# Hybrid encoder block on one Trainium2 core: channel layout at the head, forget gate behind the gate chunks, gate stores on GpSimd, two gate chunks moved out of attention

## The chip, the cores and the metric

The kernel runs on one core of one Trainium2 chip. The core has five engines, each with an instruction stream of its own: TensorE (PE: matrix products, with a separate slot PEld for loading weights), VectorE (DVE), ScalarE (ACT), GpSimd (POOL) and SyncE (SP). They work on an on-chip buffer and on accumulators; data come and go through DMA queues, which any of SP, ACT and POOL can feed. The metric is the time of one execution on the device in microseconds (us); lower is better. A measurement gives the median of several executions.

## The reference

One block of a streaming encoder, 1,024 tokens behind 16 learned ones ("meta"), so 1,040 positions of 1,024 channels, in float32. What matters here, cut from the reference:

```python
h = concatenate([meta, x], axis=1)                      # (1, 1040, 1024)
xn = _rmsnorm(h, norm_mix_g)                            # x * rsqrt(mean(x^2) + eps) * g
proj = xn @ w_in                                        # 1024 -> 512+512+512+8+512+2048
q, k, v, f_logit, u, gates = split(proj, SPLITS)
y_a = _forgetting_attention(q, k, v, f_logit, b_forget) @ w_attn_out    # 8 heads of 64
z   = gelu(_s5(u, ...))                                 # diagonal complex state space model, 32 groups of 16
zg  = z @ w_glu
y_s = zg[..., :1024] * sigmoid(zg[..., 1024:])
g   = sigmoid(gates)
h   = h + (g[..., :1024] * y_a + g[..., 1024:] * y_s) @ w_o
h   = h + _conv_ffn(_rmsnorm(h, norm_ffn_g), ...)       # 1024 -> 5632, conv of width 3, silu gate, 2816 -> 1024
out = _rmsnorm(h, norm_final_g)[:, 16:]
```

The attention adds F[t] - F[s] to its scores, where F is the running sum of log sigmoid(f_logit + b_forget): that is the forget gate. The meta tokens are dropped from the output.

## The kernel before, in words

**Precision.** TensorE multiplies in a rounded 32-bit format. Every operand is split into a high part and a low remainder, and each product is the sum of three: high by high, high by low, low by high (lines L159 to L161 in `dense_steps`, L327 to L329 in `part`). So a product over 1,024 channels is 8 blocks of 128 channels (KD = 8) times 3 matmuls.

**Stages, in the order of time.** (1) The head: the normalised tokens as features `xhi`, `xlo` (128 channels by position, 8 such blocks), and beside them the projection U for the state space model. (2) The state space model (`ssm`, four quarters of its 32 groups) with eight gate chunks as TensorE's filling. (3) Queries and keys of head pair 0 (`project_qk`), the forget gate (`forget`), the forms of z and the GLU (`load_z`, L219 in the helper for its seven products). (4) Values and the attention, four pairs of heads. (5) Merge, output product, convolutional FFN and last norm; nothing of the change touches these.

**The head.** U has 512 rows (four m of 128) over 1,040 positions, cut into blocks of columns `UBLK` = 272, 256, 256, 256. Block 0 comes from the host in channel layout (`x0t`, channels on partitions) and without the norm: its features are x times the channel's weight `g1T`, and the tokens' norm factor is multiplied in behind the product, on `us` (for which three factor vectors are spread over the partitions by transposes). All other tiles of 128 tokens are loaded in token layout (`load_x`), squared and summed on ScalarE (`norm_factor`), multiplied on VectorE by factor and weight (`features`, L340), transposed on TensorE (L191, eight transposes a tile), and then cut into high (ScalarE, L193) and low parts (VectorE, L129). Block 0's own positions are normalised in this way a second time, later, so that `xhi`, `xlo` can serve the other projections. The weights of U are cut in L355 (`uh`) and the line behind it (`ul`). The results are stored to `u_d` (L394): for odd m by GpSimd, for even m by SP, eight DMAs each.

**The state space model.** `ssm` computes its constants in long rows of small products on VectorE (L1453, L1456, L1459), then for each quarter the tables Gm, Kt, Tm, Vm and Wi: Gm on VectorE, Kt by TensorE from Gm (L1692), Wi by transposes of Vm that ScalarE copies (L1714). The chain of a quarter loads U from `u_d`, multiplies by Wi (L1730), scans, and stores Y to `y_d`. The constants are tied behind the feature product called `ready`.

**Gate chunks.** A chunk is 128 of the 2,048 gate rows: 3 blocks of 342 positions times 24 matmuls, 72 in all. Chunks 8 to 15 belong to the state space branch and are computed in stage 2, chunks 0 to 7 to attention. The weights of chunk 8 have places of their own (`gate0`, shown as g, g0 and the like). For a chunk of stage 2 (`wchunk(act=True)`) GpSimd issues the load, ScalarE casts the high part (L146) and writes its negative as the low one, and GpSimd issues a DMA (L136, `lo_by_dma`) that loads the weights once more and adds them to it. The sigmoids go to `g_d` by a DMA that ScalarE issues (L444).

**Order.** The body is written as a program; a scheduler places instructions on each engine, and `after(a, b)` pins a behind b on the order alone, without a semaphore. DMAs of one engine's queue are issued in that engine's order. Attention (`GA`, `fill`, `HOOKS`) spreads the filling of a pair evenly over its score and value steps: the next pair's queries and keys (2 x 3 x 24 matmuls) and `GA[pair]` gate chunks (72 each), here 2, 1, 1 and 3; the last of the eight is computed behind it. These chunks take tanh, GpSimd's affine step and a store by SP.

**The forget gate.** Its weights are 8 columns (`wf`, high and low side by side in 64 columns). SP issues their load behind the 32 loads of z, GpSimd cuts them (its subtraction is recorded at L129), and three blocks of 16 matmuls (L518) follow the queries and keys. ScalarE, VectorE and GpSimd then turn them into F, which is stored to `f_d` and loaded by the attention.

Of the kernel before, what the change touches and what calls it, by code (L numbers as in the profile page):

```python
# [50 lines left out]
def block_kernel(ctx, tc, x, meta, g1, x0t, g1t, w_q, w_k, w_v, w_f, w_u, w_g, b_f, w_ao, lam_d, bw_d, cw_d,  # L51
# [118 lines left out]
    def norm_factor(pl, src, n, bufs=10, sq=None):  # L170
# [3 lines left out]
        S.activation(sq[:n], src, AF.Square, accum_out=ss[:n])  # L174
        va = pl.tile([P, 1], F, tag="vr", name="vr", bufs=3)
        V.tensor_scalar(va[:n], ss[:n], 1.0 / D, EPS, ALU.mult, ALU.add)
# [110 lines left out]
    xa = [sp.tile([P, 4, UN], F, tag="tq", name="xa", bufs=3) for _ in range(2)]  # L287
    g1T = n1.tile([P, KD], F, name="g1T")
    S.dma_start(g1T, g1t)
    S.dma_start(xm, meta)  # L290
# [9 lines left out]
    for j in range(4):  # L300
        load(xa[j // 2][:, 2 * (j % 2):2 * (j % 2) + 2], x0t[:, 2 * j:2 * j + 2])
        load(uraw[j], w_u[:, 2 * j:2 * j + 2])
    xts = [sp.tile([P, D], F, tag=tag, name="xt", bufs=n) for tag, n in (("Wi", 2), ("Gm", 2), ("sy", 3)) for _ in range(n)]
    g1B = xts.pop(4)
    g1_load = S.dma_start(g1B, g1.partition_broadcast(P))

    place = dict(zip((3, 4, 1, 2, 5, 6), xts))
    place[0] = xm

    def load_x(i):  # L310
        load(place[i], x[P * (i - 1):P * i])

    for i in range(1, 7):
        load_x(i)
# [19 lines left out]
    def factors(i):  # L334
        n = TILES[i][1]
        return norm_factor(n1, place[i][:n], n)

    def features(i, rs, behind=None):
        t, n = TILES[i]
        xn = V.scalar_tensor_tensor(out=place[i][:n], in0=place[i][:n], scalar=rs[:n], in1=g1B[:n],  # L340
                                    op0=ALU.mult, op1=ALU.mult)
# [5 lines left out]
    for j in range(4):  # L347
        for k in (2 * j, 2 * j + 1):
            src, hi = xa[j // 2][:, k % 4], xhi[:, k, :UN]
            cp_ = S.activation(hi, src, AF.Copy, scale=g1T[:, k:k + 1])  # L350
            if k == 1:
                after(g1_load, cp_)
            V.scalar_tensor_tensor(out=xlo[:, k, :UN], in0=src, scalar=g1T[:, k:k + 1], in1=hi.bitcast(F),
                                   op0=ALU.mult, op1=ALU.subtract)
        S.copy(uh[j], uraw[j])  # L355
        split_lo(V, ul[j], uraw[j], uh[j])
        for m in range(4):
            for k in (2 * j, 2 * j + 1):
                part(first[m], m, k, 0, UN)
    for i in (7, 8):  # L360
        place[i] = sp.tile([P, D], F, tag="Tm", name="xt", bufs=2)
        load_x(i)

    rs0 = [factors(i) for i in range(3)]
    tp = t_ps()
    for i, rs in enumerate(rs0):
        t, n = TILES[i]
        rb = sp.tile([P, P], F, tag="wi", name="rb", bufs=2)
        V.tensor_copy(rb[:n], rs[:n].broadcast_to([n, P]))
        PE.transpose(tp[:, t:t + n], rb[:n], ident[:n, :n])  # L370
    rsB = sp.tile([P, UN], F, tag="wr", name="rsB", bufs=2)
    S.copy(rsB, tp[:, :UN])
    for i in (3, 4):
        ready = features(i, factors(i))
    n_log = len(ssm_log)
    for m in range(4):
        V.tensor_tensor(us[m][:, :, :UN // CH], by_chunks(first[m][:, :UN]), by_chunks(rsB), ALU.mult)

    for b, (t, n) in enumerate(UBLK[1:]):
        if b:  # L380
            for i in (3 + 2 * b, 4 + 2 * b):
                last = features(i, factors(i))
        for m in range(4):
            ps = mm_ps()
            for k in range(KD):
                part(ps, m, k, t, n)
            S.copy(us[m][:, :, t // CH:(t + n) // CH], by_chunks(ps[:, :n]))
        if b == 2:
            for i in range(3):
                features(i, rs0[i], last)  # L390
# [34 lines left out]

    st_g = ExitStack()
    gp_ = pool(st_g, "gates", side="right")

    okeep = {}

    def gate_chunk(i, pl, tanh):
# [3 lines left out]
        for t, n in QBLK:  # L435
# [5 lines left out]
            else:  # L441
                gs = pl.tile([P, LQ // 3], F, tag="gs", name="gs", bufs=2)
                S.activation(gs, ps[:, :n], AF.Sigmoid)
                S.dma_start(g_d[P * i:P * i + P, t:t + n], gs)  # L444
# [7 lines left out]
    for i in range(KD, 2 * KD):  # L452
# [3 lines left out]
    st_f = ExitStack()  # L456
    fp = pool(st_f, "fgate", side="right")
    fraw = fp.tile([P, KD, H], F, name="fraw")
    wf = fp.tile([P, KD, 64], R, name="wf")
    bf = fp.tile([H, 1], F, name="bf")  # L460

    def forget_w():
        SY.dma_start(fraw, w_f)
        SY.dma_start(bf, b_f.unsqueeze(1))
        GP.memset(wf.bitcast(F), 0.0)
        GP.tensor_scalar(wf[:, :, :H], fraw, 1.0, 0.0, ALU.mult, ALU.add)
        split_lo(GP, wf[:, :, 32:32 + H], fraw, wf[:, :, :H])

# [42 lines left out]
    def forget():  # L511

        fl_ = gz.tile([P, L], F, tag="gl", name="fl_", bufs=2)[:H]
        fx = gz.tile([P, L], F, tag="gl", name="fx", bufs=2)[:H]
        for t, n in BLK:
            ps = mm_ps()
            for i in range(KD):
                PE.matmul(ps[:64, :n], wf[:, i, :], xhi[:, i, t:t + n], start=(i == 0), stop=False)  # L518
                PE.matmul(ps[:64, :n], wf[:, i, :], xlo[:, i, t:t + n], start=False, stop=(i == KD - 1))
            S.copy(fx[:, t:t + n], ps[32:32 + H, :n])  # L520
            V.scalar_tensor_tensor(out=fl_[:, t:t + n], in0=ps[:H, :n], scalar=bf, in1=fx[:, t:t + n],
                                   op0=ALU.add, op1=ALU.add)
        V.scalar_tensor_tensor(out=fx, in0=fl_, scalar=-1.0, in1=fl_, op0=ALU.mult, op1=ALU.max)
        S.activation(fx, fx, AF.Exp, scale=-1.0)
        S.activation(fx, fx, AF.Ln, bias=one[:H])
        V.scalar_tensor_tensor(out=fx, in0=fl_, scalar=0.0, in1=fx, op0=ALU.min, op1=ALU.subtract)
        V.tensor_tensor_scan(fl_, one[:H].broadcast_to([H, L]), fx, 0.0, ALU.mult, ALU.add)
        GP.tensor_scalar(fx, fl_, -8.0, 0.0, ALU.mult, ALU.add)
        SY.dma_start(f_d, fx)
        if "f_d" in dbg:  # L530
            SY.dma_start(dbg["f_d"], fx)

# [3 lines left out]
    def load_z():  # L536
        zts = []
        for m in range(4):
# [3 lines left out]
            for g in range(GQ):  # L542
                SY.dma_start(zt[GC * g:GC * g + GC], ym[g])
# [62 lines left out]
    forget_w()  # L606
    qk = qk_tiles(0)
    run(project_qk(0, qk))
    forget()
    st_f.close()  # L610
# [173 lines left out]
    GA = [2, 1, 1, 3]  # L784
# [39 lines left out]
    done = 0  # L824
# [620 lines left out]
def ssm(tc, after, sp, s_ps, ident, u_d, y_d, lam_d, bw_d, cw_d, d_sk, l_dt):  # L1445
# [27 lines left out]
    S.dma_start(ldt, l_dt.partition_broadcast(P))  # L1473

    lam = sm([P, 2, G])
    S.dma_start(lam, lam_d)
# [8 lines left out]
    def rest():  # L1485
# [234 lines left out]
        def chain(qt):  # L1720
# [54 lines left out]
            S.dma_start(y_d[qt], Y)  # L1775
# [61 lines left out]
```

## Time and profile before

| | us |
|---|---|
| median of 3 runs | 1488.93 |
| the runs | 1488.93, 1492.47, 1485.58 |
| the profiled execution: its span | 1485.7 |
| stage 1, 0 to 73.5 | 73.5 |
| stage 2, 73.5 to 195.4 | 121.9 |
| pair 0, queries and keys, and forget gate, 195.4 to 238.0 | 42.6 |
| z and GLU, 238.0 to 325.0 | 87.0 |
| values and what precedes the first scores, 325.0 to 440.5 | 115.5 |
| pairs 0 to 3 of attention | 68.7, 66.8, 65.5, 65.5 |
| the rest, 707.0 to 1485.7 | 778.7 |

The span, from the first to the last instruction of the profiled execution, lies 3.2 us under the median of the runs and inside their spread; differences in the trace are set against this span.

How the rows are read. A row of the timeline is: start in us, duration in us, engine, line, operation, output<-inputs, partitions by elements, count, and in brackets the idle time before it with what ended it. Matmuls overlap, so the pitch between two starts is what one costs, not its duration. A group row is: line, engine, operation, names, shape, count | busy us, mean ns of one | idle time before. A row of stretches is: from:to, length, then the busy time (and instructions) of PE, PEld, DVE, ACT, POOL, then the granted clock of TensorE (1.00 is full), the DMA engines' mean busy share, and GB/s. A row of waits is: who <- what it waited for: us in total, times, longest. A row of DMAs is: output<-input, queue, operation, count, KB each, median us from issue to landing.

### The profile page before, as it was taken

To read this page: it belongs to the slowest core of one execution; us is meant where nothing else is said; L and a number is where in the kernel's file an instruction comes from. 1 tells how busy PE (TensorE), PEld (TensorE's weight loads), DVE (VectorE), ACT (ScalarE), POOL (GpSimd) and SP (SyncE) were. 2 spreads that over 40 slices of the span, in tenths; PEclk is the share of its full clock that TensorE was granted. 3 is DMA by queue.
4 is the path that set the end of the run, shared out by engine and by line. 5 is a ranking of instruction groups with operands and counts; after the bars stand their busy time and mean duration, and the time that the engine had idled before them with its cause. 6 is when DMAs were issued, how large, how long until landed. Compare 5 with 4: busy or idle time off the path is not lost. (4 is left out here: it accounts for less than half of the span.)

```text
span 1485.7 us, 26584 instructions
## 1 busy us (share of the span) xinstructions
PE 1440.4 (97%) x9712; PEld 1358.8 (91%) x9712; DVE 1071.4 (72%) x2173; ACT 712.2 (48%) x1384; POOL 742.1 (50%) x850
## 2 busy tenths in 40 slices
PE   7999997999999999999999999999999999998997
PEld 7989996998899999999888999999999999777886
DVE  6879648881566676647468987888877776788785
ACT  6434675541555665543546534444444445543433
POOL 1311125752456465524863144455544426789766
PEclk9999999999999999999999999999999999999999
DMA  6366571551127342047885135676653215765513
GB/s 246 86 157 157 128 163 50 177 160 43 48 79 178 93 111 90 26 148 256 257 158 185 57 109 141 178 199 188 174 143 100 84 57 180 286 203 148 168 40 114
DMA packets 91032, 206.72 MB, mean 139 GB/s; under 512 B 14651, under 2 KB 25531, under 8 KB 90517
## 3 DMA queue, kind: packets, MB, share of 16 engines
q1 hardware_dynamic: 69380, 159.73, 32.9%
q0 software_dynamic: 15296, 34.63, 13.2%
q10 hardware_dynamic: 6224, 10.65, 1.9%
q8 instruction: 77, 1.26, 0.3%
q14 instruction: 55, 0.44, 0.1%
HBM read 165.90 MB, written 69.35 MB: 158 GB/s over the span
## 5 line engine op out<-in xcount | busy, mean ns | idle before, releaser
L159 PE MATMUL mm<-xhi,whi 128*128 128x342 f32 (+2 forms) x488 | 159.4, 327 | 1.0 <-DVE q L129 1.0
L161 PE MATMUL mm<-xhi,wlo 128*128 128x342 f32 (+2 forms) x488 | 158.3, 325 | 0.0
L160 PE MATMUL mm<-xlo,whi 128*128 128x342 f32 (+2 forms) x488 | 157.7, 324 | 0.0
L1079 POOL TENSOR_TENSOR ov<-ov,og 128x1024 f32<-128x1024 f32 x21 | 51.1, 2434 | 125.6 <-ACT og L1078 121.7
L129 DVE TENSOR_TENSOR sw<-sf,sw 128x512 fp32r<-128x512 f32 x72 | 66.6, 925 | 50.0 <-ACT sw L1070 49.8
L1070 ACT CAST sw<-sf 128x512 fp32r<-128x512 f32 x72 | 44.9, 624 | 106.2 <-POOL sf L1196 74.5
L159 PEld LDWEIGHTS mm<-xhi,whi 128*128 128x128 f32 x488 | 91.9, 188 | 2.1 <-PE sp L714 0.8
L161 PEld LDWEIGHTS mm<-xhi,wlo 128*128 128x128 f32 x488 | 91.8, 188 | 0.3
L160 PEld LDWEIGHTS mm<-xlo,whi 128*128 128x128 f32 x488 | 91.9, 188 | 0.2
L763 ACT CAST th<-tp 128x256 fp32r<-128x256 f32 (+3 forms) x120 | 56.2, 472 | 62.5 <-PE tp L756 30.1
L129 DVE TENSOR_TENSOR tl<-tp,th 128x256 fp32r<-128x256 f32 (+3 forms) x120 | 65.2, 547 | 25.1 <-ACT th L763 23.7
L1196 POOL TENSOR_TENSOR sf<-raw,sf 128x512 f32<-128x512 f32 x36 | 59.1, 1641 | 44.8 <-DVE sw L129 44.7
L1196 POOL TENSOR_TENSOR sf<-raw 128x512 f32<-128x512 f32 x36 | 48.0, 1332 | 66.9 <-DMA raw<-in_w_up_dram 35.9
L221 PE MATMUL mm<-xhi,sw 128*128 128x258 f32 (+1 forms) x288 | 81.0, 281 | 0.0
L219 PE MATMUL mm<-xhi,sw 128*128 128x258 f32 (+1 forms) x288 | 80.8, 281 | 0.0
L220 PE MATMUL mm<-xlo,sw 128*128 128x258 f32 (+1 forms) x288 | 80.7, 280 | 0.0
L728 POOL TENSOR_SCALAR pt<-pt,nm 128x144 f32<-128x144 f32 (+4 forms) x72 | 51.8, 731 | 48.5 <-DVE nm L727 47.5
L1248 DVE SCALAR_TENSOR_TENSOR ov<-hv,cwt,ov 128x1024 f32<-128x1024 f32 x36 | 72.5, 2014 | 0.1
L1070 ACT CAST sw<-raw 128x512 fp32r<-128x512 f32 x70 | 43.0, 621 | 53.3 <-PE sp L221 25.5
L726 ACT ACTIVATE pt<-pt,nm 128x144 f32<-128x144 f32 (+4 forms) x72 | 52.9, 735 | 26.1 <-DVE nm L725 25.7
L719 DVE CUSTOM_DVE_ANT_0 pt<-sp,fb 128x328 f32<-128x328 f32 (+8 forms) x112 | 46.4, 430 | 20.0 <-PE sp L714 11.1
L756 PE MATMUL tp<-ident,pt 128*128 128x128 f32 (+1 forms) x360 | 58.3, 270 | 0.1
(708 smaller groups left out, 5702.1 us busy)
## 6 DMA issues: line engine op xcount, KB each, us to landing
raw<-in_w_up_dram SPq DMA_DIRECT2D x44, 512.0 KB, 3.6
t_d<-in_w_dn_dram POOLq DMA_DIRECT2D x44, 256.0 KB, 7.0
ar<-a_d SPq DMA_DIRECT2D x44, 256.0 KB, 5.1
wr<-t_d SPq DMA_DIRECT2D x44, 256.0 KB, 2.8
a_d<-ov SPq DMA_DIRECT2D x21, 512.0 KB, 2.6
wr<-in_w_dn_dram SPq DMA_DIRECT2D x33, 256.0 KB, 3.8
t_d<-in_w_dn_dram SPq DMA_DIRECT2D x22, 256.0 KB, 4.2
t_d<-t_d SPq DMA_DIRECT2D x22, 256.0 KB, 4.7
```

Source lines behind the costliest of these rows:

```text
L129: return eng.tensor_tensor(out_, src, hi.bitcast(F), ALU.subtract)
L159: yield PE.matmul(ps, whi[:, i, :], ahi[:, i], start=(i == 0), stop=False)
L160: yield PE.matmul(ps, whi[:, i, :], alo[:, i], start=False, stop=False)
L161: yield PE.matmul(ps, wlo[:, i, :], ahi[:, i], start=False, stop=(i == k - 1))
L219: PE.matmul(ps, a[0][:, i], bh, start=(i == 0 and not joins), stop=False, skip_group_check=True)
L220: PE.matmul(ps, a[0][:, i], bl, start=False, stop=False, skip_group_check=True)
L221: PE.matmul(ps, a[1][:, i], bh, start=False, stop=(i == kh - 1), skip_group_check=True)
L756: PE.transpose(tp[:kn, o:o + n], p_[:n, k0:k0 + kn], ident[:n, :n])
L763: S.copy(th[:kn, z:tw], tp[:kn, z:tw])
L1070: S.copy(hi, src)
L1196: sums.append(GP.tensor_tensor(f_, a, b, op))
L1248: V.scalar_tensor_tensor(out=o, in0=h_[:, j:SEQ + j], scalar=cwc(j, m), in1=o, op0=ALU.mult, op1=ALU.add)
```

## The change

It has four parts.

1. *The head in channel layout.* The host hands over all of x in channel layout too, by blocks of U's columns (`xbt`). Tokens are no longer transposed. The token tiles are still loaded, but only for the norm factors; each factor is spread over 128 columns by VectorE and turned by one transpose a tile, and ScalarE copies the result to `spread[b]`. For blocks 2 and 3 VectorE multiplies the whole block by `spread` ahead of the features (`normed_features`, two products of 4 x 256 columns); blocks 0 and 1 go through U without the norm, which is multiplied in on `us` behind it, and are normed and cut a second time later. The first weights and channels come in smaller pieces (`FIRST`). `ready`, behind which the constants of the state space model are pinned, is now the last feature of block 1's second pass.
2. *The forget gate* is loaded by GpSimd early in stage 2 and computed behind the gate chunks, ahead of pair 0's queries and keys; its store goes to GpSimd.
3. *GpSimd's queue* takes over the stores of the sigmoids, of Y, half of the loads of z for m = 3, and three small loads at the start.
4. *Two of attention's gate chunks* (0 and 1) are computed in stage 2, with sigmoid, behind chunks 8 to 15 (`AHEAD` = 2), and `GA` goes from 2, 1, 1, 3 to 1, 1, 0, 3.

```diff
-    S.dma_start(xm, meta)
+    GP.dma_start(xm, meta)
...
+    FIRST = [(0, 1), (1, 1), (2, 2), (4, 2), (6, 2)]
+    for k, n in FIRST:
+        load(xT[0][k // 4][:, k % 4:k % 4 + n], x0t[:, k:k + n])
+        load(uraw[k // 2][:, k % 2:k % 2 + n], w_u[:, k:k + n])
+
+    def load_block(b, tag):
+        xT[b] = [sp.tile([P, 4, UBLK[b][1]], F, tag=tag, name="xT", bufs=2) for _ in range(2)]
+        for h_ in range(2):
+            load(xT[b][h_], xbt[b - 1, :, 4 * h_:4 * h_ + 4])
...
-    def features(i, rs, behind=None):
-        t, n = TILES[i]
-        xn = V.scalar_tensor_tensor(out=place[i][:n], in0=place[i][:n], scalar=rs[:n], in1=g1B[:n],
-                                    op0=ALU.mult, op1=ALU.mult)
-        if behind is not None:
-            after(xn, behind)
-        return to_feature(place[i], n, xhi, xlo, t)[-1]
+    TB = [(0, 1, 2), (3, 4), (5, 6), (7, 8)]
...
+    def factors(b):
+        tp = t_ps()
+        t0, n_ = UBLK[b]
+        for i in TB[b]:
+            t, n = TILES[i]
+            rs = norm_factor(n1, place[i][:n], n, behind=head[0])
+            rb = rbs[:n, i % 3]
+            V.tensor_copy(rb, rs[:n].broadcast_to([n, P]))
+            PE.transpose(tp[:, t - t0:t - t0 + n], rb, ident[:n, :n])
+        S.copy(spread[b], tp[:, :n_])
+
+    def features(b, k):
+        t, n = UBLK[b]
+        src, hi = xT[b][k // 4][:, k % 4], xhi[:, k, t:t + n]
+        cp_ = S.activation(hi, src, AF.Copy, scale=g1T[:, k:k + 1])
+        cut = V.scalar_tensor_tensor(out=xlo[:, k, t:t + n], in0=src, scalar=g1T[:, k:k + 1], in1=hi.bitcast(F),
+                                     op0=ALU.mult, op1=ALU.subtract)
+        return cp_, cut
+
+    def normed_features(b):
+        t, n = UBLK[b]
+        for q in range(2):
+            V.tensor_tensor(xT[b][q], xT[b][q], spread[b].unsqueeze(1).broadcast_to([P, 4, n]), ALU.mult)
+        return [features(b, k)[1] for k in range(KD)][-1]
...
+    for m in range(4):
+        S.copy(us_part(0, m), by_chunks(first[m][:, :UN]))
+    for k in range(KD):
+        features(1, k)
+    for b in (2, 3):
+        factors(b)
+    for m in range(4):
+        ps = u_product(1, m)
+        S.copy(us_part(1, m), by_chunks(ps[:, :UBLK[1][1]]))
+    for b in (2, 3):
+        last = normed_features(b)
+        if b == 3:
+            for q in (0, 1):
+                factors(q)
+            n_log = len(ssm_log)
+            for q in (0, 1):
+                ready = normed_features(q)
         for m in range(4):
+            ps = u_product(b, m)
+            S.copy(us_part(b, m), by_chunks(ps[:, :UBLK[b][1]]))
+    for m in range(4):
+        ub = us[m][:, :, :rs01.shape[1] // CH]
+        V.tensor_tensor(ub, ub, by_chunks(rs01), ALU.mult)
...
+    GP.memset(wf.bitcast(F), 0.0)
+    for ld in (GP.dma_start(fraw, w_f), GP.dma_start(bf, b_f.unsqueeze(1))):
+        after(ld, late[0])
+    GP.tensor_scalar(wf[:, :, :H], fraw, 1.0, 0.0, ALU.mult, ALU.add)
+    split_lo(GP, wf[:, :, 32:32 + H], fraw, wf[:, :, :H])
...
-                S.dma_start(g_d[P * i:P * i + P, t:t + n], gs)
+                GP.dma_start(g_d[P * i:P * i + P, t:t + n], gs)
...
-    for i in range(KD, 2 * KD):
+    for i in [*range(KD, 2 * KD), *range(AHEAD)]:
         run(gate_chunk(i, gp_, False))
...
+    fw = pool(st_f, "fwork", side="right")
+    fl_, fx = (fw.tile([H, L], F, name=nm) for nm in ("fl_", "fx"))
+    forget()
+    st_f.close()
...
-                SY.dma_start(zt[GC * g:GC * g + GC], ym[g])
+                (GP if m == 3 and g % 2 else SY).dma_start(zt[GC * g:GC * g + GC], ym[g])
...
     T4 = load_z()
-    forget_w()
     qk = qk_tiles(0)
     run(project_qk(0, qk))
-    forget()
-    st_f.close()
...
-    GA = [2, 1, 1, 3]
+    GA = [1, 1, 0, 3]
...
-    done = 0
+    done = AHEAD
...
-    S.dma_start(ldt, l_dt.partition_broadcast(P))
+    GP.dma_start(ldt, l_dt.partition_broadcast(P))
...
-    S.dma_start(lam, lam_d)
+    GP.dma_start(lam, lam_d)
...
-            S.dma_start(y_d[qt], Y)
+            GP.dma_start(y_d[qt], Y)
```

More of the change, by code (lines that the diff above doesn't have):

```diff
@@ L173, in norm_factor @@
         ss = pl.tile([P, 1], F, tag="ss", name="ss", bufs=3)
[L174 removed]
+        sa = S.activation(sq[:n], src, AF.Square, accum_out=ss[:n])
+        if behind is not None:
+            after(sa, behind)
         va = pl.tile([P, 1], F, tag="vr", name="vr", bufs=3)
@@ L347, in block_kernel @@
[L347 to L356, printed above, removed]
+    head = []
@@ L509, in zblock @@
         return [t_[:, 2 * r:2 * r + 2, TH * h_:TH * h_ + TH] for t_ in (zhi, zlo)]
[L511 to L531, printed above, removed]
     def fold(t_):
```

115 lines of the change are left out of this document (60 added, 55 removed).

## The prediction

> **What bounds the kernel now.** I read the page first, then the table of TensorE's waits, then the busy table by stretches of time, and last the timelines of the head (0 to 100 us).
>
> ```profile
> span 1485.7 us, 26584 instructions
> PE 1440.4 (97%) x9712; PEld 1358.8 (91%) x9712; DVE 1071.4 (72%) x2173; ACT 712.2 (48%) x1384; POOL 742.1 (50%) x850
> ```
>
> TensorE is busy for 1440.4 of 1485.7 us. So a change can pay only by removing TensorE work, by removing part of its 45.3 us of idle time, or by sparing it time at a lowered clock. Its waits (us in total, times, longest):
>
> ```profile
> PE mm L327 <- ACT uh L355: 7.3, 1, 7.3
> PE sp L191 <- DVE vr L176: 3.1, 1, 3.1
> PE mm L518 <- POOL wf L129: 2.9, 1, 2.9
> PE sp L1730 <- ACT Wi L1714: 2.7, 1, 2.7
> PE sp L191 <- DVE xlo L129: 1.7, 1, 1.7
> ...
> PE mm L219 <- DVE kl L129: 0.9, 1, 0.9
> ```
>
> Five of them lie where the change works: the start, two waits of the head's transposes, the wait for the forget gate's weights, and one of the SSM. What follows them is seen in the stretches (busy us of each engine, then the granted clock, DMA share, GB/s):
>
> ```profile
> 25.00:30.00 5.00, 3.79 (x17) 3.57 (x18) 5.00 (x9) 4.07 (x8) 2.59 (x3) 0.54 0.22 83
> 70.00:75.00 5.00, 3.08 (x23) 2.64 (x21) 4.42 (x7) 3.15 (x8) 2.29 (x6) 1.00 0.90 197
> 90.00:95.00 5.00, 2.28 (x14) 2.17 (x14) 0.66 (x2) 1.07 (x2) 0.15 (x2) 0.87 0.77 257
> 95.00:100.00 5.00, 5.00 (x32) 4.64 (x32) 4.83 (x10) 3.98 (x11) 0.00 (x0) 0.79 0.19 48
> 225.00:230.00 5.00, 2.38 (x11) 2.34 (x12) 4.92 (x6) 1.41 (x3) 5.00 (x5) 0.68 0.02 5
> 230.00:235.00 5.00, 5.00 (x23) 3.98 (x22) 4.92 (x6) 3.52 (x8) 2.57 (x4) 0.63 0.00 0
> ```
>
> After the waits of 3.1, 2.7 and 2.9 us the granted clock is 0.54, 0.79 and 0.63; after the wait of 1.7 us it stays 1.00. A wait near 3 us is therefore paid twice.
>
> **Part 1, the head.** TensorE's rows there:
>
> ```profile
> 22.05 0.60 PE L191 MATMUL sp<-ident,xt 128*128 128x128 f32 x4
> 22.48 0.60 PE L191 MATMUL tp<-ident,xt 128*128 128x128 f32 x4
> 68.53 0.28 PE L328 MATMUL po<-xlo,uh 128*128 128x256 f32 x1
> 68.65 0.28 PE L329 MATMUL po<-xhi,ul 128*128 128x256 f32 x1
> 73.53 0.58 PE L159 MATMUL mm<-xhi,g 128*128 128x342 f32 x2 [0.24 <-ACT xhi L193]
> 77.34 1.05 PE L1692 MATMUL sp<-Gm,sm 128*16 128x128 f32 x8
> 79.19 0.58 PE L160 MATMUL mm<-xlo,g 128*128 128x342 f32 x2
> ```
>
> Four transposes take 0.43 us (22.05 to 22.48), a 256-column product 0.12 (68.53 to 68.65), a gate product of 342 columns, by its width, 0.16. The change drops 72 transposes of data (64 wide ones, 64 x 0.108 = 6.9 us, and 8 small ones, 0.6) and adds six of a spread factor (0.7): 6.8 us less work. The waits of 3.1 and 1.7 us go with them, and the slow clock behind the first. The first operands come in smaller pieces: one feature and half a cast in place of two features and a cast, worth about 1 us of ScalarE, and the load itself is smaller; I estimate a start at 5.8 instead of 7.3. Block 0, over now at 22.05, then ends near 20.5; three blocks of 96 products (11.5 each) and the six transposes bring the last U product to about 56, against 68.7 now, and 73.5 for the first gate product behind the old transposes. That is 17 us, if TensorE could go on.
>
> I do not think it can. In the changed program as built, three things must come before the point that in the old kernel is row 79.19 (first table products L1692 done, 22 gate products before them, 30 in the new order). Prices:
>
> ```profile
> 5.46 0.91 DVE L353 SCALAR_TENSOR_TENSOR xlo<-xa,g1T,xhi 128x272 fp32r<-128x272 f32 x2 [4.07 <-ACT xhi L350]
> 77.85 1.22 DVE L1456 TENSOR_TENSOR Vm<-sm,sm 128x1024 f32<-128x1024 f32 x1
> L340 DVE SCALAR_TENSOR_TENSOR xt<-xt,rs 128x1024 f32<-128x1024 f32 x3 | 3.7, 1266 | 0.0
> L129 DVE TENSOR_TENSOR xlo<-sp,xhi 128x512 fp32r<-128x512 f32 (+1 forms) x5 | 3.0, 593 | 2.9 <-ACT xhi L193 2.9
> L129 DVE TENSOR_TENSOR xlo<-tp,xhi 128x512 fp32r<-128x512 f32 (+1 forms) x4 | 2.4, 590 | 0.0
> 35.40:73.47 38.07, 35.69 (x300) 34.64 (x298) 30.50 (x138) 15.09 (x30) 12.09 (x30) 1.00 0.32 80
> L340 DVE SCALAR_TENSOR_TENSOR xm<-xm,rs,xt 16x1024 f32<-16x1024 f32 x1 | 1.3, 1262 | 0.0
> 64.41 0.91 POOL L136 DMA_DIRECT2D g<-in_w_g_dram  x1 [5.07 <-ACT usb L387]
> 64.99 4.05 POOL L394 DMA_DIRECT2D u_d<-usb  x7
> g<-in_w_g_dram POOLq DMA_DIRECT2D x1, 512.0 KB, 7.4
> u_d<-usb POOLq DMA_DIRECT2D x7, 65.0 KB, 7.4
> wlo<-in_w_g_dram POOLq DMA_DIRECT2D x2, 512.0 KB, 10.1
> ```
>
> (1) VectorE. ScalarE spreads the factor of block 0 only after its copies of block 2, which TensorE ends near 44. From there VectorE has four norm products (1.22, the row 77.85 of the same shape), four products on U (0.62, half of that) and 16 cuts (0.43: the two of 272 columns take 0.91): 4.9 + 2.5 + 6.9 = 14.3, so it is done near 58.5. Only then do the SSM constants begin, which now fill its gaps from 35.4 on. The four group rows are of the stretch 35.40 to 73.47, at whose end the first table now stands: of its 30.5 busy us, 10.4 are features, so constants and first table take about 20. The table then stands at 79, 5.5 later than now.
>
> (2) The first gate chunk's low weights. GpSimd's queue holds, in order, eight stores of U for m=1 (ready near 51.5; 4.05 us for seven), two weight loads, then the accumulating load of the low part. The loads wait for an earlier store's semaphore, 7.4 us after its issue, so the accumulation leaves near 60 and lands 7.4 to 10.1 us later: 68 to 70. Until then TensorE has two gate products to do. The 30 products then take 4.8 us and some 2.4 more at the low clock: 76.
>
> (3) The low weights of chunk 8 (gate0) stand behind eight more stores (m=3) and the load of that chunk itself: load near 70, there at 75, two ScalarE passes to 77, accumulation landed near 85 (bounds 80.8, where only (1) decides, and 90, with 10.1 us for every landing). TensorE needs them right behind the first table products.
>
> So TensorE passes the mark at 85 instead of 79.2, loses some 2.5 us more to the clock, and has 8 x 0.16 = 1.3 us of gate work in hand: -7.0 us (bounds -0.4 and -12). The head's 17 us are gone.
>
> **Part 2, the SSM stage and the forget gate.** ScalarE's rows show what held the 2.7 us wait:
>
> ```profile
> 90.62 1.53 ACTq L444 DMA_DIRECT2D g_d<-gs  x2
> 92.19 0.59 ACT L1714 COPY Wi<-sp 128x512 f32<-128x512 f32 x1 [8.10 <-DMA U<-u_d]
> ```
>
> Its gate stores waited 8.1 us for the semaphore of the U loads, and the copy of Wi stood behind them. With the stores on GpSimd, and U stored before 70, that wait goes: 2.7 + 1.7 at the low clock (clock 0.87 and 0.79 in the two stretches) = 4.4. The forget weights are loaded long before, so the wait on wf goes too: 2.9 + 3.0 (0.68 and 0.63, less the wait itself) = 5.9. Together +10.3. The gate products moved here, 144 x 0.16 = 22.6 us, are the same there as here. They stand between the SSM's end and the GLU, so the z forms, which now end with TensorE waiting (0.9 us on kl and more soon after), get 20 us of cover: +2.
>
> The Trainium skill (TensorE: Matmul & The Clock Gate, section on HAM oscillation) says the clock is lost by idle gaps above about 3.4 us. By that the gaps of 2.7 and 2.9 us cost only themselves, part 2 were worth 7.6 instead of 12.3, and the sum below would be -1.4. The rows have the clock at 0.79 and 0.63 behind them, so they decide.
>
> **Part 3, attention.** Pair 2 keeps no gate chunk.
>
> ```profile
> 509.20:576.00 66.80, 66.48 (x470) 64.93 (x467) 45.98 (x197) 39.97 (x97) 37.02 (x79) 1.00 0.32 88
> ```
>
> The pair would go from 66.8 to 55.5 us if TensorE stays the bound; VectorE's 46.0 us would be 83% of that. No row shows so thin a filling. Bounds: nothing, or the whole chunk (11.3). I take 2, nearer to nothing, since 83% is short of full.
>
> **Sum:** -7.0 + 10.3 + 2 - 2 = 3.3 us gained, 1482.4 for the profiled execution, whose span lies 3.2 under the median of the runs; against that median 1485.6. About 0.5% (7.4 us) is what a measurement can tell from no change.
>
> **The rivals.** A, the gate weights come in time: GpSimd's issues and landings overlap better than I queued them, only VectorE decides, and pair 2 hides its thinning. Then -0.4 + 10.3 + 2 = 12 us gained: 1477. For it: the old accumulation left within 0.6 us of the store after it, and the traffic of 59 to 75 is thinner than that of 73 to 93. Against: each load waits for a semaphore used before.
>
> B, slower: GpSimd's queue now carries weight loads, low parts, gate stores and y stores in one line.
>
> ```profile
> 107.71 1.05 ACT L146 CAST whi<-raw 128x1024 fp32r<-128x1024 f32 x1 [3.14 <-PE mm L160]
> 111.34 0.90 POOL L136 DMA_DIRECT2D wlo<-in_w_g_dram  x1 [1.70 <-ACT wlo L135]
> DMA to landing us min/median/max: 6.4/6.9/11.5
> ```
>
> A chunk's low part is there about 10.2 us after its high copy begins (3.6 + 6.5), and a chunk of 72 products lasts 11.3. A store that waits more than 1.1 us for its sigmoid or for Y ahead of the load makes the next chunk late, with the clock lost each time. Three chunks at 2.8 + 1.7: 13.5, so 1499.
>
> C, the Trainium skill (SBUF — State Buffer, section Who interferes with whom) has VectorE and GpSimd share a port pair that one of them locks. As a mechanism here, the some 20 issues ahead of gate0's low part go one by one while VectorE runs its products: at the 0.91 us that the issue at 64.41 lasted instead of 0.58, 20 x 0.33 = 6.6 us, mark at 92, 1492. Against it: seven stores went out in 4.05 us beside a busy VectorE.
>
> D, pair 2 becomes bound by its softmax chain: 9.3 us more, 1495.
>
> **How the numbers follow.** Forecast 0.38, A 0.35, B 0.15, C 0.06, D 0.06. Faster by over 0.5% (under 1481.5): A but for its slower end (0.32), and 0.06 of the forecast's: 0.38. Slower (over 1496.4): B, and the ends of the forecast, C and D, 0.08: 0.23. The rest, 0.39, is within. The range reaches from A with 5 us more (the head's full gain kept) to B: 1472 to 1500; the forecast's own is 1480 to 1491.
>
> **What would show it.** Right: no transposes of data, last U product near 56; TensorE idle near 58 to 68 and again before the first table and chunk 8's low weights, granted clock under 1 between 65 and 90; no wait for wf; no 8 us stall on ScalarE; pair 2 near 57 us. Wrong: gate products running on from 58 without a gap (A), or waits on wlo in later chunks between 110 and 220 (B).

## The result, and the profile after

The changed kernel takes 1505.12 us (median; 1502.89 to 1510.77) against 1487.84 for the kernel before: a ratio of 1.0115 (95% interval 1.0091 to 1.0138). It is 17 us slower; the forecast was 1485.6, with a range up to 1500. The profiled execution of after has a span of 1503.4, so 17.7 us more than that of before.

The head of the page of after (busy us by engine):

```profile
span 1503.4 us, 26562 instructions
PE 1444.0 (96%) x9646; PEld 1357.1 (90%) x9646; DVE 1081.8 (72%) x2201; ACT 725.4 (48%) x1418; POOL 757.5 (50%) x892
```

TensorE has 66 instructions fewer and is yet busy 3.6 us longer: "busy" counts slow products too. Its idle time grew from 45.3 to 59.4 us. The table of TensorE's waits (total, times, longest) says where:

```profile
PE po L161 <- DMA wlo<-in_w_g_dram: 12.0, 1, 12.0
PE mm L334 <- ACT uh L392: 6.3, 2, 5.7
PE sp L1722 <- DVE Gm L1486: 4.3, 1, 4.3
...
PE mm L159 <- ACT g L434: 3.0, 1, 3.0
...
PE sp L743 <- DVE mx L749: 2.5, 2, 2.0
```

The waits of the head's transposes, for wf and for Wi are gone, as forecast. In their place stand the weights of chunk 9 (12.0) and chunk 8 (3.0), the first table (4.3), and, lower down, a wait inside attention. To see what each is worth, the two traces are compared at points where TensorE has done the same work. The times are starts or ends of rows on TensorE. "Gate products in hand" are those that after has done at that point beyond what before has done; one is worth 0.157 us, a chunk of 72 of them 11.3 us. In the last column plus is slower.

| point | before | after | later by | gate products in hand | net change since the point above |
|---|---|---|---|---|---|
| last U product | 68.9 | 57.2 | -11.7 | | |
| first table products done | 79.3 | 88.6 | +9.3 | 7 (1.1 us) | **+8.2** for the head |
| first GLU product | 238.0 | 258.3 | +20.3 | 144 (22.6 us) | **-10.5** for stage 2 and the forget gate |
| first product of the values | 325.8 | 348.7 | +22.9 | 144 | **+2.7** for the GLU |
| last score product of pair 3 | 642.0 | 655.9 | +14.0 | none | **+13.6** for attention |
| last product | 1477.8 | 1496.2 | +18.4 | | **+4.4** for the rest |

With -0.7 for what follows the last product the sum is 17.7. The head and stage 2 came out within 1.2 us of the prediction. Attention came out 11.6 us worse, the GLU 4.7 us worse, and the 4.4 us of the rest were not forecast at all.

**The head.** TensorE's timeline between the last U product and the first table (start, duration, and in brackets the idle time and its releaser), and GpSimd's in the same stretch:

```profile
58.55 0.42 PE L159 MATMUL po<-xhi,whi 128*128 128x342 f32 x1 [1.36 <-ACT usb L422]
59.20 0.42 PE L160 MATMUL po<-xlo,whi 128*128 128x342 f32 x1 [0.23 <-DVE xlo L367]
71.58 0.65 PE L161 MATMUL po<-xhi,wlo 128*128 128x342 f32 x1 [11.96 <-DMA wlo<-in_w_g_dram]
79.63 0.42 PE L159 MATMUL mm<-xhi,g 128*128 128x342 f32 x1 [2.98 <-ACT g L434]
85.13 1.89 PE L1722 MATMUL sp<-Gm,sm 128*16 128x128 f32 x8 [4.29 <-DVE Gm L1486]
```

```profile
55.47 4.26 POOL L429 DMA_DIRECT2D u_d<-usb  x8 [11.80 <-ACT usb L422]
59.72 0.58 POOL L140 DMA_DIRECT2D raw<-in_w_g_dram  x1
60.61 0.55 POOL L140 DMA_DIRECT2D raw<-in_w_g_dram  x1
61.67 0.91 POOL L136 DMA_DIRECT2D wlo<-in_w_g_dram  x1 [0.51 <-DMA u_d<-usb]
...
73.21 0.57 POOL L433 DMA_DIRECT2D g<-in_w_g_dram  x1 [0.86 <-DVE sm L1486]
```

Chunk 9's low part leaves behind eight stores of U and two loads, at 61.67, and lands 9.9 us later. Chunk 8's own weights are only asked for at 73.21, when VectorE's features and GpSimd's second batch of stores are done.

**The GLU.** ScalarE's timeline in after shows the forget gate's copy (L509) and then z's casts (L581):

```profile
234.27 0.38 ACT L509 COPY fx<-mm 8x272 f32<-8x272 f32 x1 [4.13 <-DMA g_d<-gs]
...
248.51 6.82 ACT L581 CAST zhi<-zt 128x520 fp32r<-128x520 f32 x4
```

z had been loaded by 216.4 (the expectation of e2, further down, says 214); its casts stand on ScalarE behind the forget gate's copies and activations, so they begin at 248.5, where the kernel before had the first at 205.7. The GLU starts into waits, with the clock at 0.73 and 0.58 (after the clock: DMA share, GB/s):

```profile
260.00:265.00 5.00, 2.35 (x8) 1.87 (x8) 4.89 (x9) 3.72 (x8) 4.47 (x2) 0.73 0.09 16
265.00:270.00 5.00, 4.24 (x22) 3.93 (x22) 4.91 (x7) 4.26 (x12) 4.33 (x5) 0.58 0.56 159
```

**Attention.** One correction to the table at the head of this document: by the loads of the forget factors, the stretches from 440.5 on are pairs 1, 2 and 3 and what follows them. Pair 0 is what comes before 440.6. The row 509.20 to 576.00, which the prediction costs as pair 2, is pair 2 by this count too. The four pairs (from the first low-part score product of a pair, L714 before and L744 after, to that of the next pair, pair 3 to its last), first of before, then of after:

```profile
381.27:440.58 59.31, 57.47 (x387) 55.20 (x385) 38.89 (x178) 34.61 (x85) 34.11 (x72) 1.00 0.16 47
440.58:509.30 68.72, 68.33 (x480) 66.49 (x479) 45.50 (x196) 39.86 (x98) 39.25 (x81) 1.00 0.58 150
509.30:576.06 66.76, 66.44 (x469) 64.89 (x467) 45.94 (x197) 39.97 (x97) 36.98 (x79) 1.00 0.32 88
576.06:641.97 65.91, 65.65 (x466) 64.28 (x464) 41.21 (x189) 37.14 (x90) 39.45 (x76) 1.00 0.19 61
```

```profile
404.23:459.00 54.77, 51.01 (x322) 47.62 (x321) 37.23 (x176) 33.39 (x82) 29.61 (x68) 0.94 0.11 36
459.00:526.74 67.74, 67.28 (x472) 65.34 (x470) 46.23 (x198) 40.55 (x98) 39.40 (x81) 1.00 0.57 148
526.74:586.20 59.46, 57.63 (x405) 54.61 (x402) 41.55 (x192) 35.47 (x88) 33.55 (x76) 1.00 0.33 90
586.20:655.94 69.74, 67.63 (x458) 65.27 (x457) 44.09 (x193) 39.78 (x97) 39.27 (x75) 0.98 0.15 50
```

Pair 0 gave up 11.3 us of products and got 4.5 shorter: 6.8 lost. Pair 2 gave up as much and got 7.3 shorter: 4.0 lost. Pair 3 kept its three chunks and got 3.8 longer, pair 1 kept its one and got 1.0 shorter. None of the other engines is full in any of them: VectorE is at 37.2 of 54.8 us in pair 0. What shows in place of the filling is the latency of the softmax chain. The longest stretch without a filling product (a gate product or one of the next queries and keys), from one start to the next, grew from 3.0 to 5.3 us in pair 0, and in pair 3, right behind the thinned pair 2, from 3.2 to 5.65 us; in pairs 1 and 2 it stayed at 3.0 and 3.2. In pair 0 the products behind the first groups wait for VectorE's maximum (2.5 us in the table of waits), and the clock falls:

```profile
405.00:410.00 5.00, 2.75 (x12) 2.20 (x13) 3.03 (x29) 3.57 (x12) 3.36 (x12) 0.91 0.01 2
410.00:415.00 5.00, 5.00 (x16) 3.78 (x16) 2.56 (x13) 2.16 (x8) 2.52 (x9) 0.50 0.02 2
```

### The profile page after: what moved, and what is told of

Its sections match the earlier page's. It is cut to its first block, busy times and chain, and to the rows that moved or that the text cites. A ratio compares the mean times of both kernels' runs of the same rounds, so it can differ in the third digit from the quotient of the medians.

```text
span 1503.4 us, 26562 instructions
## 1 busy us (share of the span) xinstructions
PE 1444.0 (96%) x9646; PEld 1357.1 (90%) x9646; DVE 1081.8 (72%) x2201; ACT 725.4 (48%) x1418; POOL 757.5 (50%) x892
## 5 line engine op out<-in xcount | busy, mean ns | idle before, releaser
L129 DVE TENSOR_TENSOR sw<-sf,sw 128x512 fp32r<-128x512 f32 x72 | 70.5, 979 | 51.6 <-ACT sw L1100 51.5
```

The costliest lines, as they stand in the source:

```text
L129: return eng.tensor_tensor(out_, src, hi.bitcast(F), ALU.subtract)
```

## The experiments

Each kernel's time is given as its median beside the kernel before's on the same chip, and the ratio with its interval. Gains and losses against after are differences of medians to 1505.1; the experiments ran on three chips, and by the ratios the gains of e1 to e4 are each about 1 us smaller (13.8, 4.6, 13.5 and 3.1), uncertain by some 4 us.

**e1: the two chunks back in attention.**

```diff
-    AHEAD = 2
+    AHEAD = 0
-    GA = [1, 1, 0, 3]
+    GA = [2, 1, 1, 3]
```

> The changed kernel with its two gate chunks put back into attention (AHEAD = 0, GA = 2, 1, 1, 3); head, forget gate and stores stay changed. Theory N (thinned pairs): in the changed kernel attention, from the end of the GLU on, got only 9.0 us shorter for 22.5 us of gate products taken out, so 13.5 us were lost there to waits and to the clock. With the chunks back, the pairs have their old lengths (59.3, 68.7, 66.8, 65.9 us) and the kernel takes 1491.5 (1505.1 - 13.5). Rival H (the loss is the head's, the pairs are bound by something the chunks don't touch): 1503 to 1507. Rival S (stage 2 needs the two chunks as filling): below N's gain by what TensorE then waits for between the end of the state space model and the GLU, 1496 to 1500.

1490.48 against 1487.30, ratio 1.0022 (1.001 to 1.0033): 14.6 us gained, where N had 13.5. The pairs have 59.4, 68.5, 66.8 and 65.9 us in its trace, their old lengths. H and S are out.

**e2: the forget gate behind the queries and keys.** The four lines from `fw = ...` to `st_f.close()` move behind `run(project_qk(0, qk))`; the two work tiles come from the pool of z (tag `gl`), as in the kernel before.

> The changed kernel with the forget gate computed behind pair 0's queries and keys again (its weights still loaded early by GpSimd). Theory Z: in the changed kernel the casts of z stand on ScalarE behind the copies of the forget gate, which wait for TensorE until 234; z was there at 214, the casts begin at 248.5, and the GLU starts into 4.9 us of waits and 3.5 us of slow clock. With the forget gate behind the queries and keys the casts run beside the last gate chunks and the waits shrink to the old kernel's or less: 5 to 8 us gained, 1497 to 1500. Rival (z forms are held by VectorE's work for queries and keys, as in the old kernel, which waits 5.35 us there at full clock): 2 to 3 us gained, 1502 to 1503. Rival, no effect: 1505.

1499.43 against 1487.30, 1.0084 (1.0063 to 1.0105): 5.7 us gained, inside Z's bounds, though the interval overlaps that of after (1.0091 to 1.0138). The casts of z begin at 232.5 in place of 248.5, beside the queries and keys. At the first product of the values the trace is 2.7 us ahead of after, which is what the move of the casts is worth there; a further 2.4 us come up in attention and 1.4 behind it, which the edit doesn't touch. The forget gate runs without a wait behind the queries and keys too, 7.9 us long (7.7 in after).

**e3: chunk 8's weights early.**

```diff
-             for dt, tag, n in ((F, "Wi", 2), (R, "sy", 3), (R, "Wi", 2))]
+             for dt, tag, n in ((F, "Tm", 2), (R, "sy", 3), (R, "Tm", 2))]
...
-    after(GP.dma_start(gate0[0], w_g[KD]), last)
+    after(GP.dma_start(gate0[0], w_g[KD]), last2)
```

with `last2` the last cut of block 2, and these lines ahead of the stores of U.

> The changed kernel with chunk 8's weights in buffers that are free 25 us earlier (those of block 2 of x), loaded behind block 2's cuts and ahead of the stores of U on GpSimd's queue; nothing else changed. Theory W (late weights): between 57.2 and 88.5 us TensorE did 30 gate products and the first table in 31.3 us, work for 6.6 us at full clock. With chunk 8 there at 57, its 72 products fill 57 to 68.5, and chunk 9's low part (landing 68 to 73) and then the table (85) follow; of the 24.7 us some 10 stay lost: 15 gained, 1490 (bounds 1483 and 1497). Rival V (VectorE's table at 85 sets the end of the stage, what is done ahead of it is missing behind it): under 3 us gained, 1502 to 1505. Rival Q (GpSimd's queue moves the wait to chunk 9): 6 gained, 1499.

1490.58 against 1487.30, 1.0024 (1.0012 to 1.0036): 14.5 gained (forecast 15). The waits for g and Gm are gone. The first table products end at 88.6, as in after, but now with 128 gate products done before them in place of 30, so what the head lacked was filling and not an earlier table. 7.1 us for chunk 9's low part stay:

```profile
PE po L161 <- DMA wlo<-in_w_g_dram: 7.1, 1, 7.1
```

**e4: all stores of U on SP.** `(GP if m % 2 else SY)` becomes `SY`.

> The changed kernel with all 32 stores of U on SP's queue, none on GpSimd's. Theory Q (the accumulating loads are late because GpSimd issues eight stores and waits for their semaphores ahead of them): chunk 9's low part leaves at 58.5 in place of 61.7 and lands at 66 in place of 71.5, chunk 8's lands some 10 us earlier; the wait of 12.0 us shrinks to 7: 5 to 8 us gained, 1497 to 1500. Rival D (the DMA engines are full there, 1.0 to 1.15 busy from 60 to 75 us, and the landing takes what it takes): under 2 us gained, 1503 to 1505. Rival (the chain of the state space model waits for U, now stored later): slower, 1507 or more.

1501.29 against 1487.30, 1.0094 (1.0073 to 1.0114): 3.8 gained, between Q and D, with an interval that overlaps that of after. The wait for wlo fell from 12.0 to 6.9, so the queue was part of it; but the scheduler's order put chunk 8 next and 7.9 us of waiting for its low part came in.

**e5, e6, e7: the three edits together,** with the chunks all in attention (e5: GA 2, 1, 1, 3), one taken from pair 2 (e6: AHEAD 1, GA 2, 1, 0, 3) or from pair 0 (e7: AHEAD 1, GA 1, 1, 1, 3).

> The three edits together: chunk 8 early (as e3), forget gate behind the queries and keys (as e2), both gate chunks back in attention (as e1). If the three losses are separate, their gains of 14.5, 5.7 and 14.6 us add up: 1470. Rival F (filling): with chunk 8 early and the two chunks gone, the gate work ends some 12 us ahead of the state space model's end near 200, and TensorE waits there unless the queries and keys fill it: 1476 to 1484.

> As e5, but with one gate chunk in stage 2, taken from pair 2 (AHEAD = 1, GA = 2, 1, 0, 3). By the changed kernel's trace pair 2 lost 4.0 us and pair 3 3.8 against e1; if both come from pair 2's missing chunk, this is 7.8 us slower than e5 (1478 where e5 is 1470); if pair 3's loss comes from elsewhere, 4 us slower. Rival F (stage 2 lacks filling): faster than e5 by up to 6 us.

> As e5, but with one gate chunk in stage 2, taken from pair 0 (AHEAD = 1, GA = 1, 1, 1, 3). Pair 0 lost 6.7 us in the changed kernel for its one chunk: 6.7 us slower than e5 (1477 where e5 is 1470), pairs 2 and 3 at 66.8 and 65.9. Rival F (stage 2 lacks filling): faster than e5 by up to 5 us.

e5: 1484.37 against 1487.28, 0.9976 (0.9965 to 0.9986). e6: 1485.70, 0.9990 (0.9975 to 1.0004). e7: 1482.21, 0.9961 (0.9946 to 0.9976). The gains of e1 to e3 do not add up (1470). e5 lies 0.4 us above rival F's bounds. Against e5, e7 is 2.2 us faster and e6 1.3 slower, both inside the intervals, so the times alone don't settle F; the traces show its mechanism. A chunk of 11.3 us put into stage 2 makes the first product of the values only 4.3 (e6) and 4.6 us (e7) later. Attention then gets 2.2 us shorter where the chunk came from pair 2 (pair 2 60.2 and pair 3 69.6, against 66.8 and 65.9 in e5) and 6.7 us where it came from pair 0 (53.8 against 59.3). In e5 the state space model ends at 202.7, the GLU starts at 222.1, and the table of waits from 200 to 340 is now led by VectorE's and ScalarE's work for the GLU (z forms and results) and for the forget gate:

```profile
PE sp L222 <- DVE z2l L129: 2.8, 1, 2.8
PE mm L221 <- ACT c L230: 2.7, 1, 2.7
PE mm L221 <- ACT ms L234: 1.4, 1, 1.4
PE mm L221 <- DVE fl__2610 L512: 1.3, 1, 1.3
```

**e8: the chunks' move alone, on the kernel before.**

> The kernel before with only the move of the two gate chunks (behind chunks 8 to 15, with sigmoid; GA = 1, 1, 0, 3). Theory N: the pairs lose the 13.5 us that they lost in the changed kernel, and the z forms get 22.5 us of cover for waits of some 5 us: 1487.3 + 13.5 - 3 = 1498 (1495 to 1502). Rival (the pairs' loss comes of the changed kernel's head or of its forget gate): 1485 to 1489.

1496.38 against 1487.28, 1.0069 (1.0042 to 1.0096): 9.1 slower, inside N's bounds. Its pairs have 54.7, 67.4, 60.8 and 69.7 us, those of after within 1.3 us, so the pairs' loss is the thinning's own, whatever the head does. This trace is of the longest of e8's five runs, 1505.85 us; the others took 1495 to 1499.

**e9, e10: the model's constants early.** e9 is e7 with

```diff
-        features(1, k)
+        early = features(1, k)[1]
...
-    after(ssm_log[n_log], ready)
+    after(ssm_log[n_log], early)
```

and e10 is e9 with the stores of U for m = 3 on SP (`m == 1` in place of `m % 2`).

> e7 (chunk 8 early, forget gate late, one gate chunk in stage 2, GA = 1, 1, 1, 3) with the constants of the state space model tied to block 1's first cuts in place of the last cut of its second pass, so that they may fill VectorE's idle time from 25 us on. Theory C (in e5 and e7 the state space model's end near 203 sets the start of the GLU, and it is late because its constants start only behind all features): the first table comes 6 to 9 us earlier (80 to 83 where e7 has it done at 89.5), the model's end too, and the GLU's waits shrink: 1474 to 1478 (e7: 1482.2). Rival U (the small operations push block 2's and 3's features back, TensorE waits in U for what it saves later): 1481 to 1486. Rival T (VectorE's later work in the model sets its end whatever the start): 1481 to 1483.

> e9 with the stores of U for m = 3 on SP's queue, so that on GpSimd's queue the accumulating load of chunk 9 stands behind one batch of eight stores, not two. In e7 TensorE waited 7.5 us for that load's landing (70 to 79) and ran at a clock of 0.51 and 0.81 after it. If the batch is what delays it, the wait falls to 2 to 4 us and the clock stays up: 4 to 7 us faster than e9. Rival D (the DMA engines are full there): within 2 us of e9.

e9: 1479.54 against 1488.20, 0.9935 (0.9914 to 0.9957): 2.7 better than e7 by the medians, 3.9 by the ratios, with intervals that overlap; theory C's bounds began at 4.2. The first table was done at 78.6 and the model at 189.6 (e7: 89.5 and 203.7), but the GLU starts at 234.6 (e7: 232.7) and only its waits shrink. e10: 1485.66, 0.9992 (0.9974 to 1.001), worse than e9. The wait for wlo is gone as meant, but the new order has the first table behind 35 more instructions of TensorE, done at 83.3, and the model ends at 197.0. Here an edit of a queue changed the order on TensorE too; the forecast looked at the queue alone.

**e11, e12: two terms of part 2, each alone on the kernel before.** e11 loads the forget weights early by GpSimd, e12 has `GP.dma_start` for the sigmoids' stores.

> The kernel before with only the forget gate's weights loaded early by GpSimd (computed where it was). Theory: the wait of 2.9 us on wf goes and with it 3.0 us at the low clock: 5.9 us faster, 1481.4. Rival (z forms and the cuts of the queries and keys end where they end, so the GLU starts no earlier; the forget gate was filling ahead of it): 0 to 2 us faster.

> The kernel before with only the stores of the sigmoids on GpSimd's queue. Theory: ScalarE's 8.1 us stall and TensorE's 2.7 us wait for Wi go, with 1.7 us of slow clock: 4.4 us faster, 1482.9. Rival (the stores delay the accumulating loads in one queue, later chunks wait): 2 to 10 us slower. Rival (the state space model's chain is bound by VectorE, the wait only moves): 0 to 1.

e11: 1488.77 against 1488.20, 0.9996 (0.9978 to 1.0013): nothing. The wait on wf is gone, and the next one stood right behind it:

```profile
PE mm L517 <- DVE kl L129: 4.1, 1, 4.1
```

By this row the forget gate's products stood still until VectorE had cut the keys, whose accumulators they take over. e12: 1485.51, 0.9973 (0.9959 to 0.9987), 2.7 gained by the medians and 4.0 by the ratio (1.9 to 6.1), so the theory's 4.4 is not contradicted. A wait of 1.8 us for U took the place of the 2.7 for Wi, and the clock stayed at 1.00.

**e13: the head by itself** (e1 and e2 together: chunks in attention, forget gate behind the queries and keys, chunk 8 as in the change).

> The changed kernel with the gate chunks back in attention (as e1) and the forget gate behind the queries and keys (as e2), chunk 8's weights as the change has them: what is left of the change is the head and GpSimd's stores and early loads. If the terms add up: 1505.1 - 14.6 - 5.7 = 1484.8. If the head by itself costs the 7.0 us of the prediction and the stores on GpSimd give back 2.7 (e12): 1491.6. Rival V (in e5, which differs from this only in chunk 8's early weights, the start of the GLU is set by the state space model's end, so the weights gain nothing here): 1484 to 1486, as e5.

1491.84 against 1485.99, 1.0031 (1.0012 to 1.0049). Neither the added-up 1484.8 nor V; the prediction's own head term with e12's 2.7 gives 1491.6. Once the chunks are back e2's move gains nothing (e1 has 1.0022), and against e5 (0.9976) chunk 8's early weights are worth 0.55% or 8 us.

**e14: only the constants early, on after.**

> The changed kernel with only the constants of the state space model tied to block 1's first cuts (as e9). Theory W (late weights hold the head of the changed kernel): the wait of 4.3 us for the first table goes, that of 12.0 us stays: 3 to 5 us faster, 1500 to 1502. Rival C (the model's late start is what costs the changed kernel its time): 8 us or more faster, below 1497. Rival U (U is pushed back): 1504 or more.

1505.61 against 1485.99, 1.0139 (1.0107 to 1.0172): no gain, which only rival U had. The table is done at 78.3, 10 us earlier, but the constants push the last features back, and the two waits take the place of the old ones:

```profile
PE sp L1722 <- DVE Gm L1486: 10.0, 1, 10.0
PE po L160 <- DVE xlo L367: 5.1, 1, 5.1
```

**e15, e16: where to take the chunk from.** e15 is e9 with AHEAD 0 and GA 2, 1, 1, 3; e16 is e9 with AHEAD 1 and GA 2, 1, 1, 2.

> e9 with both gate chunks in attention (AHEAD = 0, GA = 2, 1, 1, 3). Pair 0 gets back the 6.1 us that it lost in e9 for its chunk of 11.3 (54.1 against 59.3): 1473.4, if stage 2 has filling enough. Rival F (stage 2 lacks filling, as in e5 against e7): 1480 to 1484.

> e9 with the gate chunk of stage 2 taken from pair 3 in place of pair 0 (AHEAD = 1, GA = 2, 1, 1, 2). Pair 3 has no queries and keys to cut, so VectorE and ScalarE have least to do in it (39 and 24 us busy of 65.5 in the row that was taken for it before, which is the stretch from 641.5 on; in pair 3 itself, 576 to 642, 41 and 37): if it hides the thinning better than pair 0, which lost 6.1 us, 1474 to 1478; if it loses the same, 1479 to 1480; if its softmax chain binds, 1481 or more.

e15: 1477.13 against 1485.99, 0.9939 (0.9918 to 0.996). e16: 1475.00, 0.9923 (0.9895 to 0.9951). Both beat before and after; their intervals overlap, so the order between them, and between them and e9, is open. Pair 3 of e16:

```profile
573.32:630.06 56.74, 56.41 (x405) 54.83 (x403) 39.96 (x188) 35.71 (x87) 35.26 (x73) 1.00 0.16 52
```

It is 9.2 us shorter than in before (65.9) for the 11.3 taken out, and TensorE is idle in it for 0.3 us; pair 0 got 4.5 us shorter for the same in after, and 5.2 in e9 (54.1 against 59.3 in e15).

## Why the prediction was wrong

In this section a gain is positive, as in the prediction, so the signs are those of the table above turned round.

**Part 1, the head: the sum right, with some luck.** Forecast -7.0, measured -8.2 at the first table (23 gate products stand before it in the old order, not 22), and 4.6 us (0.31%) lost in e13, which has the head with GpSimd's stores. Start 5.8 (5.67), last U product near 56 (56.9), chunk 9's low part 68 to 70 (71.6). VectorE's terms were too small. The features were done at 61.9, not 58.5: the first norm product began at 46.1, not 44, and the products on U run over blocks 0 and 1 together, 1.16 us each where 0.62 was taken. Constants and table then took 23.2 us, not 20. The prediction let chunk 8's low part decide the point, at 85, and had the table 6 us ahead of it. The low part landed at 86.3 (it left at 80.97 and took 5.3), but the table came at 85.1, stood first in TensorE's order and decided: its products were done at 88.6. The sum came close because the table, the term that was too small, ended within 1.2 us of the low part, on which the sum rested.

**Part 2: the sum right, its reasons half.** Forecast +10.3, measured +10.5: between the first table and the GLU TensorE waits for nothing in after, at a clock of 1.00 from 90 us on. The 4.4 for the sigmoids' stores fit e12 (2.7 by the medians, 4.0 by the ratio). The 5.9 for wf do not come from the early load by itself, as e11 shows. Nor is the place ahead of the queries and keys needed for them: the forget gate takes 7.7 us there in after, against 10.5 behind a wait of 2.9 in before, but it takes 7.9 (e2) and 7.7 us (e13) without a wait behind them too. Which part of the change removes the wait for the keys that e11 and e12 have there, no run shows.

**The z forms: wrong sign, forecast +2, measured -2.7.** "They get 20 us of cover" took for granted that they would be done in that time. z was there, but on ScalarE the casts stood behind the forget gate's copies, which waited for TensorE, and these behind the two moved chunks. e2, which undoes this, is 2.7 us ahead of after at the first product of the values. In e1, without the two chunks, the casts begin at 226.7. The prediction followed the moved step along GpSimd's queue, and not along ScalarE's.

**Part 3: the step that failed.** Forecast -2, measured -13.6, and e1 gave 14.6 us back. It costed pair 2 alone, at 2; pair 2 lost 4.0. Pair 0 lost a chunk too (2 to 1) and cost most, 6.8; and pair 3 paid 3.8 because pair 2's filling no longer reached it: between 595.7 and 601.33 TensorE had no filling product. That this comes of pair 2's missing chunk, two other traces show: e6, which thins pair 2 and not pair 0, has pair 3 at 69.6, and e7, which thins pair 0 and not pair 2, at 65.9. The bound was judged by VectorE's share of busy time (83% "is short of full"). Here a chain of short steps on several engines bound by its latency, with the fullest of them, VectorE, busy for 68% of pair 0 and 70% of pair 2.

**The rivals.** D named the place, with 9.3 us in pair 2 and a chance of 0.06; it took three pairs together (14.6, less 1.0 in pair 1) to lose more than that. B's mechanism (stores late in GpSimd's queue, waits on wlo in later chunks) did not show: after 92 us no wait on wlo stands in the table. C's did not: eight stores went out in 4.26 us, 0.53 each, beside a busy VectorE.

**The rest, -4.4, was not forecast,** and lies in stages that the change doesn't touch. From the last score product of pair 3 to the last product the trace of before takes 835.9 us and that of after 840.3. The code is the same there in all experiments: e3 takes 846.1, the other fifteen 836.7 to 840.0. So before is the shortest of all eighteen; e8, e11 and e12, which are built on it, take 839.2, 837.7 and 836.9. The 4.4 us lie within what executions of the same code differ by, and a cost of the change is not shown there. One source of this spread is in the traces. A wait of 3.0 us stands at the same place in both kernels; the timeline rows and the stretches behind them, first of before, then of after:

```profile
1368.60 0.47 PE L1365 MATMUL mm<-xlo 128*128 128x512 f32 x1 [3.01 <-ACT xlo L1310]
...
1370.00:1380.00 10.00, 10.00 (x45) 8.13 (x45) 10.00 (x11) 3.23 (x6) 7.71 (x5) 1.00 1.04 318
```

```profile
1384.67 0.47 PE L1395 MATMUL mm<-xlo 128*128 128x512 f32 x1 [3.03 <-ACT xlo L1340]
...
1380.00:1390.00 10.00, 6.97 (x24) 5.26 (x23) 10.00 (x12) 5.14 (x10) 9.36 (x7) 0.83 1.06 238
```

The clock stays at 1.00 behind one and has 0.83 over 10 us behind the other, which is 1.7 us lost. What makes up the rest of the spread is open.

## What to carry to other kernels

Filling that is spread over a latency-bound loop has a price per stage: take it from where the traces show least lost (here pair 3, 2.1 of 11.3 us, against 6.8 in pair 0), and read the price from the length of each stage, not from its busy shares. Look at the stage behind it too. When a step is moved, look at the order of instructions on every engine that it runs on: what stands behind its first waiting instruction is moved with it. A gain at one end of a stage is kept only if what the next stage needs also comes earlier: the early constants alone gained nothing here (e14), and it took the early weights, the early constants, the forget gate behind the queries and keys, and the filling given back to pairs 0 and 2 to turn 1.0115 into 0.9923 (e16).

## What the hardware showed that was not expected

The wait of 3.0 us near the end cost itself alone in before and 1.7 us more in after. All eighteen traces have it at this place, 3.0 to 3.1 us long. In three of them (before, e5 and e12) the clock stayed at 1.00 behind it; in the other fifteen it was 0.69 to 0.84 over the next 10 us, so 1.6 to 3.1 us were lost. So the prediction's "paid twice" is what mostly happens, and not a rule; e12's wait of 1.8 us left the clock at 1.00. The Trainium skill (TensorE: Matmul & The Clock Gate, section What's actually happening) has the activity window of about 3.4 us run freely, with no regard to when the work starts, which agrees with the two outcomes of one wait; its limit of about 3.4 us for a gap does not agree with the clock lost after 3.0.

Between 60 and 65 us of after, the DMA engines were full at a third of the rate that they reached between 10 and 15:

```profile
10.00:15.00 5.00, 5.00 (x30) 5.00 (x30) 4.27 (x8) 4.44 (x8) 0.00 (x0) 1.00 1.03 410
...
60.00:65.00 5.00, 0.00 (x0) 0.00 (x0) 4.59 (x20) 0.00 (x0) 2.83 (x7) 0.60 1.15 133
```

By 65 us 26 of the 32 stores of U, 65 KB each, had been issued from two queues, with two loads of weights beside them. The accumulating load issued at 61.67 took 9.9 us to land, where the next one, issued at 73.77, took 7.2. Whether the small stores are what kept the rate down, no run shows.
